# Expert rows gathered by buffer alone: four row buffers, VectorE's row steps tied behind the weight splits

## The chip, the cores and the metric

The kernel runs on one core of one Trainium2 chip. The metric is the device time of one execution in microseconds (us). The time before is 3835.49 us, the median of 3 runs (3828.89 to 3838.25). Engines: TensorE (PE), VectorE (DVE), ScalarE (ACT), GpSimd (POOL) and SyncE (SP); SP, ACT and POOL also issue DMAs, each from its own queue.

## The reference

One decoder block on x of 512 tokens by 2048 features, in float32. Two token mixers run in parallel (a gated causal convolution of 31 taps, and a grouped complex state space model), are gated, merged and projected. Then comes the channel mixer, called PEER, and a final RMS norm:

```
q = h @ w_q;  s = q . sub_keys                 # 8 heads, 2 halves of 128 keys
top 16 of each half; the 256 sums; top 16 of those   -> expert ids (of 16384), gates = softmax
act = gelu(h . u_tab[expert])                  # 8 heads x 16 experts a token
out = sum over experts of gates * act * v_tab[expert]
```

Each token so picks 128 of 16384 experts. An expert is one row of 2048 numbers (8 KB) of `u_tab` and one of `v_tab`; each table has 128 MB.

## The kernel before

**Stages.** Up to about 1412 us the mixers and the routing run: weight pieces of 128x1024 (512 KB) are loaded by SP, split by ACT (high part, line 209) and DVE (low part, line 210), and multiplied by PE as three products. Then comes PEER, which treats the tokens in two ways at once.

**Dense way.** The last 352 tokens (`ND`) are multiplied with *all* experts. `dense_u(j)` makes the gelu of 128 experts' scores (`ga`, from 48 matmuls of 352 columns); `weigh(j, ga)` multiplies it on DVE by the gates of those experts, which `load_gates` brings from DRAM for four `j` at a time into one buffer `gq`, and splits the product; `dense_v(g, dc, ws)` multiplies eight such products with a quarter of the V table (96 matmuls) and DVE adds the sum to `acc`. The first 32 columns of `dense_u` (`LEAD`) run ahead and are reloaded later; after them the loop at line 1243 goes over 16 groups `g` and 4 quarters `dc`. From group 3 to 14 one pass through the inner loop, here called a step, holds two `dense_u`, two `weigh` and one `dense_v`: 192 matmuls and eight weight pieces, taken from the stream `tabs`, which loads up to six and splits up to three pieces ahead.

**Row way.** The first 160 tokens are done by rows. For each token's expert number `e`, `gather_row` has POOL issue an indirect DMA that brings 128 rows of 8 KB, one for each partition (1 MB), into a buffer of the ring `row`; DVE then takes one instruction over 128x2048: for U a product with a sum (line 1113), for V a multiply-add into the result `x` (line 1116). 128 tokens take 128 gathers for each table, and 32 tokens, four partitions to a token, 32 for each: 320 gathers in all. `gather()` is a generator, one row to a `yield`; `pump_rows(n)` advances it by n rows at four places of a step, so that the rows are spread over the dense work. In a step some six rows are taken.

**What sets the order.** The queue of each engine is fixed when the program is built. A scheduler takes the operations in the order of the program where their buffers allow, and may take a later one first. `tc.issue_after(ins)` adds an edge: what is written inside comes behind `ins`. Each queue then runs strictly in order. In the kernel before, a gather is held behind `pace[0]`, an instruction of POOL that was written shortly before it: mostly a copy of one column, `mark`, which `paced` makes from `ga` after a `dense_u` or from `acc` after a `dense_v` (line 1142):

```
        with after(pace[0]):
            nc.gpsimd.indirect_dma_start(out=g, ...)
...
            while len(live) < 2:
                ahead()
```

Three row buffers (`NROW`) hold the row in use and two begun ahead. The ring of `ga` has four buffers (`NR`). The row ring also serves the row way's `xt` and `gain`, the residual `res` in group 0 and `sqj` at the end. `dynamic_dma_scratch_size` reserves 8192 bytes of each partition for the descriptors of POOL's DMAs.

Of the kernel before, what the change touches and what calls it, by code (L numbers as in the profile page):

```python
# [38 lines left out]
LAG = 11  # L39
GM = 1  # L40
TAIL = 5
NR = 4
NROW = 3
RLEAD = 0.8
RV = 0.8
REND = 4.5
# [109 lines left out]
def kernel(ctx, tc, xT, vecs, cst, w_in, conv_w_out, w_vg, w_out, w_q, keysT,  # L156
# [47 lines left out]
        return pp.tile([128, T], F32, name="ps", tag="proj", bufs=4)  # L204

    pace = [None]

    def split(hi, lo, src, eng=None):
        ins = nc.scalar.copy(hi, src).ins  # L209
        low = (eng or nc.vector).tensor_tensor(lo, src, hi.bitcast(F32), op=ALU.subtract)  # L210
        if eng is nc.gpsimd:
            pace[0] = low.ins
        return ins

    rings = {"raw": [(wp, 4)], "hi": [(wp, 3)], "lo": [(wp, 3)]}
# [763 lines left out]

    def weigh(j, ga):  # L980

        if j % QG == 0:
            load_gates(j // QG)
        if j < LEAD:
            ga = gars.pop(j) if j in gars else reload(j)
        g3 = ga.rearrange("p (b t) -> p b t", t=32)
        nc.vector.tensor_tensor(g3, gq[0][:, :, j % QG, :], g3, op=ALU.mult)  # L987
        p = wgp[j // GRP % 2]
        wh, wl = (p.tile([128, ND], F32R, name=n, tag="w") for n in ("wh", "wl"))
        split(wh, wl, ga)  # L990
        return wh, wl

    def reload(j):
# [60 lines left out]

    def gather_row(tab, ids, e):
        g = row("grow")
        with after(pace[0]):
            nc.gpsimd.indirect_dma_start(out=g, out_offset=None, in_=tab,
                                         in_offset=bass.IndirectOffsetOnAxis(ap=ids[:, e:e + 1], axis=0))
        return g  # L1060

    def gather():
        blocks = [(0, GA, eidx, gta, HK, rt[:, 0:1]),
                  (GA, GB, eidb, gtb, HK // REP, rtb)]
        passes = [(b, tab) for b in blocks for tab in (peer_u, peer_v)]
        todo = [(tab, b[2], e) for b, tab in passes for e in range(b[4])]
        live, xt, gain = [], [], []

        def ahead():
            if todo:  # L1070
                live.append(gather_row(*todo.pop(0)))

        def load(b):
            t0, n = b[:2]
            x = row("xt")
            for c in range(128 // n):
                nc.sync.dma_start(x[c * n:(c + 1) * n], d_xr[t0:t0 + n])
            xt.append(x)

        def load_gain():  # L1080
            gain.append(row("gain"))
            nc.gpsimd.dma_start(gain[0], gffn[None, :].to_broadcast([128, D]))

        def turn(scale):
            x2 = rowp.tile([128, D], F32, name="rows0", tag="rows", bufs=1)
            nc.scalar.activation(x2, xt.pop(), AF.Copy, scale=scale)
            return x2

        load(blocks[0])
        load_gain()  # L1090
        for _ in range(3):
            yield
        for p, (b, tab) in enumerate(passes):
            t0, n, ids, gates, steps, r = b
            nxt = passes[p + 1] if p + 1 < len(passes) else (None, None)
            if tab is peer_u:
                x = turn(r)
                ahead()
                _mul(nc, x, x, gain.pop())
            else:  # L1100
                x = turn(float(n) / 128)
            while len(live) < 2:
                ahead()
            for i in range(steps):
                if i == steps - 2 and nxt[0]:
                    load(nxt[0])
                elif i == steps - 1 and nxt[1] is peer_u:
                    load_gain()
                else:
                    ahead()  # L1110
                g = live.pop(0)
                if tab is peer_u:
                    nc.vector.scalar_tensor_tensor(g, g, 1.0, x, op0=ALU.mult, op1=ALU.mult,  # L1113
                                                   accum_out=act[:, i:i + 1])
                else:
                    nc.vector.scalar_tensor_tensor(x, g, act[:, i:i + 1], x, op0=ALU.mult, op1=ALU.add)  # L1116
                yield
            if tab is peer_u:
                with after(last_ga[0]):
                    nc.scalar.activation(act[:, :steps], act[:, :steps], AF.Gelu_apprx_tanh)  # L1120
                _mul(nc, act[:, :steps], act[:, :steps], gates)
                continue
            if n < 128:
                for _ in range(3):
                    yield
                y = row("ysum")
                for q in range(4):
                    pt = ps_v()
                    nc.tensor.matmul(pt[:n], sel, x[:, q * 512:(q + 1) * 512], start=True, stop=True)  # L1129
                    nc.scalar.copy(y[:n, q * 512:(q + 1) * 512], pt[:n])  # L1130
                x = y
            nc.sync.dma_start(out[t0:t0 + n, :], row_norm(x[:n], gfin))
        yield
# [2 lines left out]
    gth = gather()  # L1136
    gi = [0, 0.0]

    def paced(ap):

        mark = con2.tile([128, 1], F32, name="mark", tag="mark", bufs=2)
        pace[0] = nc.gpsimd.tensor_copy(mark, ap[:, 0:1]).ins  # L1142

    def pump_rows(n):
        gi[1] += n
        while gi[0] < gi[1]:
# [4 lines left out]
    for j in range(LEAD):  # L1151
        if j >= LEAD - 4:
            jn = 2 * (j - LEAD + 4)
            gars.update((i, reload(i)) for i in (jn, jn + 1))
        if j == 0:
            rows_load()
        if j in (4, 6):
            rows_turn()
        ga = dense_u(j, gate_steps if j >= LAG else None)
        if j == LAG - 1:  # L1160
            transp_routes()
        if j >= LEAD - 5:
            paced(ga)
            pump_rows(RLEAD)
        if j >= LEAD - 4:
            ws_next += [weigh(jn, None), weigh(jn + 1, None)]
# [50 lines left out]
    def dense_v(g, dc, ws):  # L1217
        pcs = []
        pairs = [ps_v((2, 512)) for _ in range(2)]
        pvs = [pairs[i // 2][:, i % 2, :ND] for i in range(4)]  # L1220
        last = range(GRP - 2, GRP)
        order = [(e, i) for e in range(GRP - 2) for i in range(4)] + [(e, i) for i in range(4) for e in last]
        for at, (e, i) in enumerate(order):
            if at == 16 and g == NE // GRP - 1 and dc:
                turn_out(dc - 1)
            if e // 2 == len(pcs):
                pcs.append(tabs.take())
            hi, lo = pcs[e // 2]
            wh, wl = ws[e]
            s = slice(e % 2 * 512 + i * 128, e % 2 * 512 + (i + 1) * 128)  # L1230
            nc.tensor.matmul(pvs[i], hi[:, s], wh, start=e == 0, stop=False)  # L1231
            nc.tensor.matmul(pvs[i], hi[:, s], wl, start=False, stop=False)  # L1232
            nc.tensor.matmul(pvs[i], lo[:, s], wh, start=False, stop=e == GRP - 1)  # L1233
        for h in range(2):
            a, pv = acc[:, 4 * dc + 2 * h:4 * dc + 2 * h + 2], pairs[h][:, :, :ND]
            _add(nc, a, pv, a if g else res[dc][:, 2 * h:2 * h + 2])
        paced(acc[:, 4 * dc + 3])
        if g == NE // GRP - 1 and dc == 3:
            turn_out(dc)

# [2 lines left out]
    for g in range(ngrp):  # L1243
        ws = ws_next
        ws_next = []
        for dc in range(4):
            if g == ngrp - 1 and dc == 3:
                for _ in gth:
                    pass
            if g == ngrp - 1 and dc == 0:  # L1250
                hst.close()
                op = ctx.enter_context(tc.tile_pool(name="op", bufs=1, reuse_waits="tile"))
                tail["ost"] = op.tile([128, len(BLKS), D], F32, name="ost")
                tail["sqs"] = op.tile([128, len(BLKS), 4], F32, name="sqs")
                tail["gfb"] = op.tile([128, D], F32, name="gfb")
                nc.gpsimd.dma_start(tail["gfb"], gfin[None, :].to_broadcast([128, D]))
            for jn in range((g + 1) * GRP + 2 * dc, (g + 1) * GRP + 2 * dc + 2):
                if jn < NE:
                    ga = None
                    if jn >= LEAD:  # L1260
                        ga = dense_u(jn)
                        paced(ga)
                    ws_next.append(weigh(jn, ga))
                    if jn >= LEAD:
                        pump_rows(rate / 2)
            n = RV / 4 * (3 + (g > 0)) if (g + 1) * GRP < LEAD else rate / 2 if g < ngrp - 1 else REND / 2 if dc < 3 else 0
            if g == 0 and dc < 3:
                load_res()
            pump_rows(n)
            dense_v(g, dc, ws)  # L1270
            pump_rows(n)
# [83 lines left out]
```

## Time and profile before

| | |
|---|---|
| median of 3 runs | 3835.49 us |
| the profiled execution: its own time | 3822.91 us |
| its span, first to last instruction | 3821.1 us |
| busy: PE, DVE, ACT, POOL | 3514.3, 2712.8, 1256.4, 1004.8 us |
| PE, DVE share of the span | 92%, 71% |
| DMA queue of SP: share of 16 engines' span, MB | 35.8%, 437.58 |
| DMA queue of POOL | 27.3%, 396.12 |

The profile is of one execution. A row with a wait names the engine, what it writes and the line, then after an arrow what ended the wait, and the sum, count and longest wait. In a row for a stretch, PEclk is the granted TensorE clock as a share of full speed, and the DMA share is the mean busy share of the 16 DMA engines. Busy shares over the whole span hide that the stages have different limits.

### The profile page before, as it was taken

The page shows a single profiled execution, that of the slowest core. Times are in us where ns is not written, and L with a number is a line of the kernel's source. Part 1 is how long each engine was busy: PE and PEld are TensorE (multiplying, and loading weights), DVE is VectorE, ACT ScalarE, POOL GpSimd, SP SyncE. Part 2 cuts the span into 40 slices and gives each one's busy share as a digit, 9 for nine tenths or more (in the row PEclk, how much of TensorE's full clock was granted, in tenths as well). Part 3 has the DMA queues.
Part 4 walks back from the last instruction along what each step waited for, and adds up shares of the span by engine and source line. Part 5 has one row for each costly group of instructions (what it writes and reads, how often), then busy time and mean ns, then how long its engine had stood idle before and what let it go on. Part 6 is the DMA issues. An engine that isn't in the chain of part 4 may idle for free. (4 is left out here: it accounts for less than half of the span.)

```text
span 3821.1 us, 49889 instructions
## 1 busy us (share of the span) xinstructions
PE 3514.3 (92%) x19059; PEld 3257.5 (85%) x19059; DVE 2712.8 (71%) x4006; ACT 1256.4 (33%) x2009; POOL 1004.8 (26%) x832
## 2 busy tenths in 40 slices
PE   8999999999999999989998998988788888889877
PEld 6888888888888899988998998888788887889877
DVE  8686678985349998756667677676576666767666
ACT  4334434242323348732222222232222222232223
POOL 1100001000025452121233233333343333332331
PEclk9999999999999999999999999999899999999988
DMA  5533444344444356687678888886788767888874
GB/s 184 140 109 115 127 126 143 114 133 140 141 136 121 116 165 208 224 304 254 236 289 301 302 304 306 302 305 245 262 299 292 283 248 267 300 303 308 313 274 182
DMA packets 218863, 852.35 MB, mean 223 GB/s; under 512 B 41168, under 2 KB 58656, under 8 KB 173376
## 3 DMA queue, kind: packets, MB, share of 16 engines
q1 hardware_dynamic: 144704, 437.58, 35.8%
q0 software_dynamic: 64512, 396.12, 27.3%
q10 hardware_dynamic: 9408, 15.47, 1.1%
q8 instruction: 149, 2.44, 0.3%
q14 instruction: 90, 0.74, 0.1%
HBM read 795.23 MB, written 53.84 MB: 222 GB/s over the span
## 5 line engine op out<-in xcount | busy, mean ns | idle before, releaser
L209 ACT CAST whi<-wraw 128x1024 fp32r<-128x1024 f32 x736 | 761.6, 1049 | 1462.4 <-PE ps L269 575.0
L210 DVE TENSOR_TENSOR wlo<-wraw,whi 128x1024 fp32r<-128x1024 f32 x682 | 830.6, 1225 | 227.1 <-ACT whi L209 226.7
L1233 PE MATMUL pv<-wh,wlo 128*128 128x352 f32 x2048 | 707.2, 345 | 178.3 <-DVE wlo L210 178.2
L1231 PE MATMUL pv<-wh,whi 128*128 128x352 f32 x2048 | 704.4, 344 | 34.8 <-DVE acc L61 32.8
L270 PE MATMUL pu<-h2h,wlo 128*128 128x352 f32 x2048 | 676.0, 330 | 50.8 <-DVE wlo L210 50.8
L1232 PE MATMUL pv<-wl,whi 128*128 128x352 f32 x2048 | 696.5, 340 | 0.0
L268 PE MATMUL pu<-h2l,whi 128*128 128x352 f32 x2048 | 681.1, 333 | 1.1 <-ACT whi L209 1.1
L269 PE MATMUL pu<-h2h,whi 128*128 128x352 f32 x2048 | 668.2, 326 | 0.0
L1116 DVE SCALAR_TENSOR_TENSOR rows<-grow,act,rows 128x2048 f32<-128x2048 f32 x160 | 375.7, 2348 | 332.2 <-DMA grow<-in_peer_v_dram,eidx 282.1
L1233 PEld LDWEIGHTS pv<-wh,wlo 128*128 128x128 f32 x2048 | 417.8, 204 | 194.3 <-DVE wlo L210 194.3
L1113 DVE SCALAR_TENSOR_TENSOR grow<-grow,rows 128x2048 f32<-128x2048 f32 x160 | 366.2, 2289 | 277.3 <-DMA grow<-in_peer_u_dram,eidx 227.4
L1231 PEld LDWEIGHTS pv<-wh,whi 128*128 128x128 f32 x2048 | 418.3, 204 | 39.2 <-DVE acc L61 36.0
L270 PEld LDWEIGHTS pu<-h2h,wlo 128*128 128x128 f32 x2048 | 390.7, 191 | 58.1 <-DVE wlo L210 58.0
L1232 PEld LDWEIGHTS pv<-wl,whi 128*128 128x128 f32 x2048 | 419.0, 205 | 0.0
L268 PEld LDWEIGHTS pu<-h2l,whi 128*128 128x128 f32 x2048 | 393.3, 192 | 1.4 <-ACT whi L209 1.4
L269 PEld LDWEIGHTS pu<-h2h,whi 128*128 128x128 f32 x2048 | 391.8, 191 | 0.0
L268 PE MATMUL ps<-hl,whi 128*128 128x512 f32 x896 | 353.2, 394 | 8.7 <-ACT whi L209 8.7
L270 PE MATMUL ps<-hh,wlo 128*128 128x512 f32 x896 | 350.7, 392 | 0.5 <-DVE wlo L210 0.4
L269 PE MATMUL ps<-hh,whi 128*128 128x512 f32 x896 | 350.2, 391 | 0.0
L209 ACT CAST wh<-ga 128x352 fp32r<-128x352 f32 x96 | 46.7, 486 | 834.7 <-DVE ga L987 834.7
L1142 POOL COPY mark<-acc 128x1 f32<-128x1 f32 x64 | 84.5, 1320 | 757.2 <-DVE acc L61 757.2
L1142 POOL COPY mark<-ga 128x1 f32<-128x1 f32 x101 | 97.5, 966 | 506.5 <-ACT ga L916 492.4
(347 smaller groups left out, 5134.0 us busy)
## 6 DMA issues: line engine op xcount, KB each, us to landing
wraw<-in_peer_ut_dram SPq DMA_DIRECT2D x256, 512.0 KB
wraw<-in_peer_vt_dram SPq DMA_DIRECT2D x256, 512.0 KB
wraw<-in_w_in_dram SPq DMA_DIRECT2D x112, 512.0 KB
d_g<-stg SPq DMA_DIRECT2D x22, 1024.0 KB
gq<-d_g POOLq DMA_DIRECT2D x32, 704.0 KB, 11.1
wraw<-in_w_vg_dram SPq DMA_DIRECT2D x32, 512.0 KB
wraw<-in_w_out_dram SPq DMA_DIRECT2D x32, 512.0 KB
wraw<-in_w_q_dram SPq DMA_DIRECT2D x32, 512.0 KB
```

The lines of the kernel that those rows point to most:

```text
L209: ins = nc.scalar.copy(hi, src).ins
L210: low = (eng or nc.vector).tensor_tensor(lo, src, hi.bitcast(F32), op=ALU.subtract)
L268: nc.tensor.matmul(ps, hi[:, sl], al[k], start=k == 0, stop=False)
L269: nc.tensor.matmul(ps, hi[:, sl], ah[k], start=False, stop=False)
L270: nc.tensor.matmul(ps, lo[:, sl], ah[k], start=False, stop=k == nk - 1)
L1113: nc.vector.scalar_tensor_tensor(g, g, 1.0, x, op0=ALU.mult, op1=ALU.mult, accum_out=act[:, i:i + 1])
L1116: nc.vector.scalar_tensor_tensor(x, g, act[:, i:i + 1], x, op0=ALU.mult, op1=ALU.add)
L1142: pace[0] = nc.gpsimd.tensor_copy(mark, ap[:, 0:1]).ins
L1231: nc.tensor.matmul(pvs[i], hi[:, s], wh, start=e == 0, stop=False)
L1232: nc.tensor.matmul(pvs[i], hi[:, s], wl, start=False, stop=False)
L1233: nc.tensor.matmul(pvs[i], lo[:, s], wh, start=False, stop=e == GRP - 1)
```

## The change

The tie `after(pace[0])` is taken off the gathers; their place in POOL's queue follows from their buffer alone. The copies `mark` and `paced` go. `NROW` becomes 4 and three rows are begun ahead. The DVE step of a row is tied behind the last low split that was written before it for DVE (`last_low`). The gates of four columns are loaded right behind the last `weigh` that uses the ones before, no longer at the first that needs them. `NR` becomes 3, and the descriptor scratch 4096 bytes.

```diff
-NR = 4
-NROW = 3
+NR = 3
+NROW = 4
...
         if eng is nc.gpsimd:
             pace[0] = low.ins
+        else:
+            last_low[0] = low.ins
...
     def weigh(j, ga):
-        if j % QG == 0:
-            load_gates(j // QG)
+        if j == 0:
+            load_gates(0)
...
         split(wh, wl, ga)
+        if j % QG == QG - 1 and j + 1 < NE:
+            load_gates(j // QG + 1)
         return wh, wl
...
         g = row("grow")
-        with after(pace[0]):
-            nc.gpsimd.indirect_dma_start(out=g, ...)
+        nc.gpsimd.indirect_dma_start(out=g, ...)
         return g
...
-            while len(live) < 2:
+            while len(live) < NROW - 1:
                 ahead()
...
-                if tab is peer_u:
-                    nc.vector.scalar_tensor_tensor(g, g, 1.0, x, ..., accum_out=act[:, i:i + 1])
-                else:
-                    nc.vector.scalar_tensor_tensor(x, g, act[:, i:i + 1], x, ...)
+                with after(last_low[0]):
+                    if tab is peer_u:
+                        nc.vector.scalar_tensor_tensor(g, g, 1.0, x, ..., accum_out=act[:, i:i + 1])
+                    else:
+                        nc.vector.scalar_tensor_tensor(x, g, act[:, i:i + 1], x, ...)
...
-    def paced(ap):
-        mark = con2.tile([128, 1], F32, name="mark", tag="mark", bufs=2)
-        pace[0] = nc.gpsimd.tensor_copy(mark, ap[:, 0:1]).ins
...
-            paced(ga)
...
-        paced(acc[:, 4 * dc + 3])
...
-                        paced(ga)
...
-    nc = _bacc.Bacc("TRN2", ..., dynamic_dma_scratch_size=8192)
+    nc = _bacc.Bacc("TRN2", ..., dynamic_dma_scratch_size=4096)
```

## Rows read from the trace of the kernel before

**Rows 1.** Stretches: us, busy us (instructions) of PE PEld DVE ACT POOL, PEclk, DMA share, GB/s.
```profile
0.00:1412.00 1412.00, 1390.62 (x6535) 1165.96 (x6536) 1063.81 (x2418) 512.92 (x810) 260.42 (x270) 1.00 0.44 134
1412.00:1691.00 279.00, 267.73 (x1830) 264.72 (x1831) 200.85 (x259) 183.19 (x496) 63.36 (x55) 0.98 0.67 229
1691.00:1887.00 196.00, 178.24 (x1043) 175.91 (x1043) 123.75 (x142) 54.10 (x64) 33.15 (x32) 0.95 0.73 249
1887.00:3722.00 1835.00, 1602.35 (x9222) 1580.33 (x9220) 1263.24 (x1112) 475.52 (x587) 628.63 (x461) 0.93 0.80 290
3722.00:3821.10 99.10, 75.37 (x434) 70.55 (x434) 61.10 (x79) 30.67 (x53) 19.26 (x15) 0.88 0.48 180
```

**Rows 2.** Waits from 1887 to 3722 us: total us, times, longest us.
```profile
POOL mark L1142 <- DVE acc L61: 581.3, 48, 18.6
POOL mark L1142 <- ACT ga L916: 464.9, 49, 13.1
...
DVE rows L1116 <- DMA grow<-in_peer_v_dram,eidx: 282.1, 47, 9.9
...
DVE grow L1113 <- DMA grow<-in_peer_u_dram,eidx: 187.7, 46, 9.6
...
PE pv L1233 <- DVE wlo L210: 177.1, 51, 6.2
...
DVE grow L1113 <- DMA grow<-in_peer_u_dram,eidb: 49.7, 12, 10.5
PE pu L270 <- DVE wlo L210: 46.5, 22, 5.4
...
DVE rows L1116 <- DMA grow<-in_peer_v_dram,eidb: 41.5, 8, 8.3
```

**Rows 3.** POOL in order of time: start us, us, engine, line, operation [wait before].
```profile
2685.45 2.11 POOL L1142 COPY mark<-ga 128x1 f32<-128x1 f32 x1 [10.21 <-ACT ga L916]
2687.71 4.91 POOL L1058 DMA_INDIRECT grow<-in_peer_v_dram,eidx  x1 [0.16 <-DVE wlo L210]
2692.93 0.94 POOL L1058 DMA_INDIRECT grow<-in_peer_v_dram,eidx  x1 [0.30 <-issue]
2694.17 0.94 POOL L1058 DMA_INDIRECT grow<-in_peer_v_dram,eidx  x1 [0.30 <-issue]
2695.11 1.14 POOL L978 DMA_DIRECT2D gq<-d_g  x1
```

**Rows 4.** DVE in the same stretch: the row step that waits.
```profile
2701.41 2.35 DVE L1116 SCALAR_TENSOR_TENSOR rows<-grow,act,rows 128x2048 f32<-128x2048 f32 x1 [8.47 <-DMA grow<-in_peer_v_dram,eidx]
```

**Rows 5.** Groups by line, 1887 to 3722 us: count | busy us, mean ns | wait before.
```profile
L1116 DVE SCALAR_TENSOR_TENSOR rows<-grow,act,rows 128x2048 f32<-128x2048 f32 x150 | 352.2, 2348 | 324.3 <-DMA grow<-in_peer_v_dram,eidx 282.1 <-DMA grow<-in_peer_v_dram,eidb 41.5 <-ACT rows L1086 0.2
L1113 DVE SCALAR_TENSOR_TENSOR grow<-grow,rows 128x2048 f32<-128x2048 f32 x140 | 320.4, 2288 | 237.3 <-DMA grow<-in_peer_u_dram,eidx 187.7 <-DMA grow<-in_peer_u_dram,eidb 49.7
```

**Rows 6.** Two single steps, columns as in the first group.
```profile
3426.00:3460.00 34.00, 29.17 (x164) 28.59 (x163) 29.57 (x29) 7.50 (x10) 11.19 (x9) 0.90 0.95 354
3460.00:3497.00 37.00, 36.78 (x227) 36.49 (x226) 25.76 (x27) 11.90 (x15) 13.47 (x10) 1.00 0.82 298
```

**Rows 7.** Line 1058, 1887 to 3722 us: durations in ns (min/median/max); issue to landing.
```profile
L1058 POOL DMA_INDIRECT grow<-in_peer_v_dram,eidb x23: 945/973/6062, 3571.6 to 3709.7; - x23
...
DMA to landing us min/median/max: 5.7/9.4/15.1
```

**Rows 8.** Waits of SP's queue, whole span.
```profile
SPq L245 <- DVE wlo L210: 2038.4, 474, 14.0
...
SPq L995 <- DVE wl L210: 19.4, 10, 6.5
```

**Rows 9.** Groups by line, 1691 to 1887 us.
```profile
L1231 PE MATMUL pv<-wh,whi 128*128 128x352 f32 x347 | 117.4, 338 | 17.8 <-DVE acc L61 17.8
...
L987 DVE TENSOR_TENSOR gar<-gq,gar 128x352 f32<-128x352 f32 x20 | 9.8, 522 | 8.3 <-DMA gq<-d_g 8.3
```

More of the change, by code (lines that the diff above doesn't have):

```diff
@@ L206 @@
     pace = [None]
+    last_low = [None]
     def split(hi, lo, src, eng=None):
@@ L1056, in gather_row @@
         g = row("grow")
-        with after(pace[0]):
-            nc.gpsimd.indirect_dma_start(out=g, out_offset=None, in_=tab,
-                                         in_offset=bass.IndirectOffsetOnAxis(ap=ids[:, e:e + 1], axis=0))
+        nc.gpsimd.indirect_dma_start(out=g, out_offset=None, in_=tab,
+                                     in_offset=bass.IndirectOffsetOnAxis(ap=ids[:, e:e + 1], axis=0))
         return g
@@ L1111, in gather @@
                 g = live.pop(0)
-                if tab is peer_u:
-                    nc.vector.scalar_tensor_tensor(g, g, 1.0, x, op0=ALU.mult, op1=ALU.mult,
-                                                   accum_out=act[:, i:i + 1])
-                else:
-                    nc.vector.scalar_tensor_tensor(x, g, act[:, i:i + 1], x, op0=ALU.mult, op1=ALU.add)
+                with after(last_low[0]):
+                    if tab is peer_u:
+                        nc.vector.scalar_tensor_tensor(g, g, 1.0, x, op0=ALU.mult, op1=ALU.mult,
+                                                       accum_out=act[:, i:i + 1])
+                    else:
+                        nc.vector.scalar_tensor_tensor(x, g, act[:, i:i + 1], x, op0=ALU.mult, op1=ALU.add)
                 yield
@@ L1341 @@
     laid = _layout(inputs)
-    nc = _bacc.Bacc("TRN2", target_bir_lowering=False, num_devices=1, dynamic_dma_scratch_size=8192)
+    nc = _bacc.Bacc("TRN2", target_bir_lowering=False, num_devices=1, dynamic_dma_scratch_size=4096)
     arrays, args = {}, []
```

## The prediction

> **What bounds the kernel now.** I read the page's shares first: PE 92%, DVE 71%. That looks like a kernel bound by PE, but it is an average. So the second view is busy time by stretch [rows 1]. Up to 1412 us PE is busy 1390.6 of 1412.0 us at a granted clock of 1.00: nothing on the row way can help there. From 1887 to 3722 us, nearly half the span, PE is busy 1602 of 1835 us and its clock is 0.93. This is where the reader should look. The stretch holds 9222 matmuls, and a step has 192, so it holds 48 steps of 38.2 us.
>
> What would a step take if PE never waited? In one step PE was busy 36.78 of 37.00 us at full clock with 227 matmuls [rows 6]: 0.162 us each, so 192 take 31.1 us. A step therefore loses 7.1 us. The third view, who waited for whom in that stretch, says to what [rows 2]. PE waits 177.1 + 46.5 = 223.6 us for `wlo`, a low split by DVE: 4.7 us a step. The remaining 2.4 us are the clock's: it is granted at two levels, 1.2 and 2.4 GHz, the mean is 0.93 in this stretch where PE pauses often, and it was 1.00 in the step without pauses [rows 1, 6].
>
> Why is a DVE that is busy 26.3 us a step (1263.2 / 48) late? Because it also waits 282.1 + 187.7 + 49.7 + 41.5 = 561.0 us for rows to land, 11.7 us a step [rows 2]. 26.3 + 11.7 = 38.0 of 38.2 us: **DVE either works or waits for a row**, and the splits that PE needs stand behind the waiting row in its queue. It is DVE's queue that sets the step, not its work.
>
> The fourth view, POOL and DVE in order of time, shows why rows come late [rows 3, 4]. POOL waits 10.2 us for the `ga` that its mark copies, and then three gathers go out at once, at 2687.7, 2692.9 and 2694.2. DVE needs the first of them at once and stands 8.5 us until it lands, starting at 2701.4. In the 1835 us marks waited 581.3 us for `acc` and 464.9 us for `ga` [rows 2]: the gathers follow DVE's and PE's progress, DVE follows the gathers, and PE follows DVE. It is a loop with the landing time in it (median 9.4 us, longest 15.1) [rows 7].
>
> **The change, part by part.**
>
> *Gathers untied, fourth buffer.* A gather now needs only the end of the row step four before it. A step takes 290 / 48 = 6.04 rows [rows 5]. At a step of 33.4 us (below) rows come every 5.5 us, so a gather has 4 x 5.5 - 2.35 = 19.8 us before its row is wanted, and the median landing takes 9.4 us and the longest 15.1 [rows 7]. On the mean this covers the landing; two rows in a bunch eat some of the 10 us of slack. I take the 11.7 us of waiting as gone, except for what POOL itself costs.
>
> *What is late next.* Without that wait DVE needs 26.3 us and PE 31.1. But POOL's issue gets dearer as DVE pauses less. A gather takes 0.94 us when DVE stands still, and one that was issued into a run of DVE work took 4.91 [rows 3]; the longest took 6.06 [rows 7]. Suppose that POOL only gets on while DVE pauses: per step 6.04 gathers x 0.95 plus half a gates' load of 1.14 [rows 3] are 6.3 us, and 26.3 + 6.3 = 32.6 us. If issues overlapped freely the bound would be PE's 31.1; if every one took 6.06, with 0.30 between them, 6.04 x 6.36 + 0.57 = 39.0. I take 32.6: most gathers now last between the two, and a row that comes late for this reason itself makes the pause in which POOL catches up. PE then idles 1.5 us a step and not 4.7, a third, so I leave a third of the clock's loss, 0.8 us. **A step of 33.4 us**, and 48 x (38.2 - 33.4) = 230 us saved.
>
> The Trainium skill, "SBUF — State Buffer", section "SBUF: two separate sides", has a rule here that speaks against the change: a DMA from GpSimd's queue stalls, because its descriptors cannot be written, for as long as DVE runs an operation that takes both of its ports. The 4.91 us against 0.94 [rows 3] agree in direction; whether the stall is complete they do not show. By the rule no step below 32.6 us is possible, since every gather would have to be written in DVE's pauses; without it PE's 31.1 would stand and the saving would be some 330 us.
>
> *VectorE's steps behind the last split.* It costs no instruction. It puts the splits that were written before a row ahead of it, so a late row no longer holds these; up to three split pieces of 24 matmuls, 3 x 3.9 = 11.7 us, then stand ready for PE. The other side: a row that has landed waits where the split in front of it waits for `ga` or for a piece that PE still holds. Four places a step would have to cost 2.9 us each to eat the present 11.7. I take 0, as DVE has 31.1 - 26.3 = 4.8 us of slack a step, and such a wait means that DVE is ahead of PE.
>
> *Marks removed, gates' load moved.* The marks are POOL work beside everything; their cost was their wait. The gates' load (1.14 us on POOL, every second step) now stands right behind the last use of the old gates, and gathers behind it wait for a multiply of DVE. That costs at most a wait like the mark's, 10.2 us [rows 3], once in two steps, under a lead of 19.8; I take 0. In exchange the 8.3 us go that DVE waits for gates [rows 9].
>
> *Groups 0 to 2* (1691 to 1887 us). 1043 matmuls x 0.162 = 169 of 196 us, and PE waits 17.8 us for `acc` behind DVE's late rows [rows 1, 9]. Fewer rows fall here, so I take half of the 27 us lost: 13. Three `ga` buffers for four make SP wait one reload sooner; SP waited 19.4 us for these in all, off PE's path, as the weight stream waits much longer for DVE (2038 us) anyway [rows 8]. I take 0; +19 if it came on the path, or nothing.
>
> *Scratch of 4 KB.* The trace does not show how full it is. Before 1412 us PE's idle time is 21 us in all, so POOL's DMAs are hidden there; I take 0, with 20 us either way. From 1412 to 1691 and behind 3722 us (few rows left, PE busy 75 of 99) I take 0, with 20 us to be gained at most [rows 1].
>
> **Sum.** 230 + 13 = 243 us. The profiled execution took 3822.9 (span 3821.1), and becomes 3580. The median of the runs shown lies 12.6 above it, so I predict **3592 us**.
>
> **Rivals.**
>
> *PE's floor is reached.* Issues overlap well and rows are always there: a step of 31.3, 48 x 6.9 = 331, with 20 more in the groups before: 3485 us. For it: four buffers give twice the median landing time. Against it: the long issues.
>
> *The DMA engines become the bound.* A step moves 290 GB/s x 38.2 us = 11.1 MB [rows 1]; in 33.4 us that is 332 GB/s, at a share of 0.92 instead of 0.80. One step ran at 354 and 0.95, with eight rows, in 34.0 us [rows 6], but one step is no stretch, and gathers with more in flight slow the weights. If the share stops at 0.87, a step takes 38.2 x 0.80 / 0.87 = 35.1 us; 48 x 3.1 = 149, and 8 before: 3678 us.
>
> By the Trainium skill, "DMA: Bandwidth & Descriptors", section "Specifications", the HBM gives one core some 358 GB/s; an estimate by it is 11.1 / 0.358 = 31 us a step, so it would not bind above PE's floor. The 354 GB/s of that one step agree.
>
> *It doesn't do what it says.* Buffers come free in bunches, because row steps come in bunches and the gates' load holds POOL for DVE; the gathers still go out three at a time, DVE still stands for the first, and the loop closes over the buffers in place of the marks. Against it: in the waits of today [rows 2, 3] the gathers go at once when the mark is there, so their buffers were free before. Price 0: 3835.
>
> *Slower: POOL's issue becomes the bound.* With DVE nearly always at work each gather takes as long as the longest now. 39.0 us a step (above) is 0.8 over today's, so 3835 + 37 = 3872 us. It decides from a mean issue of (38.2 - 0.57) / 6.04 - 0.30 = 5.9 us. For it: 4.91 and 6.06 are there already. Against it: POOL is busy only 628.6 / 48 = 13.1 us a step, marks included [rows 1], and with every late row DVE pauses.
>
> **Chances.** Forecast (steps of 32 to 34.5 us) 0.52, PE's floor 0.13, DMA 0.19, nothing 0.07, slower 0.09. About 0.3%, some 12 us, is what a measurement of this kernel can tell from no change. Faster by more: 0.52 + 0.13 + 0.19 = 0.84; within: 0.07; slower: 0.09. The range goes from PE's floor, 3480, past the DMA case to 3730, where the bounds of 20 us each lie inside; what it leaves out is nothing, slower and a little of each end.
>
> **What would show it.** Right: between the same groups a step of 33 to 34 us; DVE's wait for rows under 3 us a step; PE's wait for `wlo` a third of 224 us, clock above 0.96; gathers spread over the step and not in threes; their median issue above 1.5 us. DMA case: a share of 0.87 to 0.9, PE and ACT waiting for `wraw`. Slower case: POOL busy over 30 us a step. I am wrong if DVE still waits 8 us for rows at one place of each step, or if it waits for the splits in front of them instead.

## The result: 3470 us, and the profile after

The changed kernel takes 3470.27 us, the median of 4 runs (3465.20 to 3472.65), beside 3832.19 us for the kernel before (4 runs). The ratio is 0.9059 (0.9030 to 0.9088): 362 us less, where I forecast 243 less and put the low end of the range at 3480. The direction was right, the size was not. The profiled execution took 3465.2 us.

The page of the kernel after, span and busy times with their shares:

```profile
span 3463.4 us, 49577 instructions
...
PE 3384.4 (98%) x19059; PEld 3151.0 (91%) x19059; DVE 2709.3 (78%) x4006; ACT 1276.2 (37%) x2009; POOL 905.3 (26%) x667
```

DVE has the same work as before (2712.8 us), in a shorter span. Busy time by stretch, columns as in [rows 1]; group 3 begins at 1886 us (before: 1887) and group 15 at 3377 (before: 3722):

```profile
1886.00:3377.00 1491.00, 1486.55 (x9219) 1486.25 (x9218) 1269.60 (x1115) 495.51 (x586) 546.26 (x318) 1.00 0.93 356
...
3377.00:3463.40 86.40, 70.65 (x430) 65.87 (x428) 59.87 (x78) 30.59 (x53) 10.82 (x8) 0.95 0.50 193
```

| | before | after | difference |
|---|---|---|---|
| up to group 3 | 1887 | 1886 | -1 |
| groups 3 to 14, 48 steps | 1835 | 1491 | -344 |
| from group 15 on | 99.1 | 86.4 | -13 |

All but 14 us of the gain lies in the 48 steps. One takes 1491 / 48 = 31.06 us, and PE is busy 30.97 of them at a clock of 1.00: it is PE's floor. The waits of that stretch, columns as in [rows 2]:

```profile
POOL grow L1062 <- DVE rows L1121: 453.4, 144, 11.8
ACT whi L210 <- PE pv L1231: 448.2, 188, 9.1
POOL grow L1062 <- DVE grow L1118: 420.2, 83, 14.4
...
DVE wlo L211 <- ACT whi L210: 169.0, 100, 2.6
...
DVE grow L1118 <- DMA grow<-in_peer_u_dram,eidb: 5.7, 3, 4.8
...
PE pv L1232 <- DVE wlo L211: 4.5, 1, 4.5
...
DVE rows L1121 <- DMA grow<-in_peer_v_dram,eidx: 2.3, 2, 1.6
```

DVE's waits for rows fell from 561.0 us to 5.7 + 2.3 = 8.0, PE's waits for `wlo` from 223.6 to 4.5 (I had left it a third). The arrows have turned: POOL waits for DVE to free a row buffer, DVE for ACT's high part, and ACT for PE to free a piece. Everybody waits for PE. POOL and then DVE in order of time, columns as in [rows 3]:

```profile
2225.98 0.94 POOL L1062 DMA_INDIRECT grow<-in_peer_u_dram,eidx  x1 [3.60 <-DVE grow L1118]
2228.99 1.68 POOL L1062 DMA_INDIRECT grow<-in_peer_u_dram,eidx  x1 [2.07 <-DVE grow L1118]
2238.23 2.75 POOL L1062 DMA_INDIRECT grow<-in_peer_u_dram,eidx  x1 [7.56 <-DVE grow L1118]
```

```profile
2226.43 2.28 DVE L1118 SCALAR_TENSOR_TENSOR grow<-grow,rows 128x2048 f32<-128x2048 f32 x1
...
2228.64 2.35 DVE L211 TENSOR_TENSOR wlo<-wraw,whi 128x1024 fp32r<-128x1024 f32 x2
2233.01 1.23 DVE L211 TENSOR_TENSOR wlo<-wraw,whi 128x1024 fp32r<-128x1024 f32 x1 [2.01 <-ACT whi L210]
2234.15 0.52 DVE L990 TENSOR_TENSOR ga<-gq,ga 128x352 f32<-128x352 f32 x1
2235.22 0.53 DVE L211 TENSOR_TENSOR wl<-ga,wh 128x352 fp32r<-128x352 f32 x1 [0.55 <-ACT wh L210]
2235.66 2.29 DVE L1118 SCALAR_TENSOR_TENSOR grow<-grow,rows 128x2048 f32<-128x2048 f32 x1
```

Each gather goes as soon as a row step has freed its buffer. On DVE the splits and the multiply of `ga` now stand in front of the next row step, and no row step waits: answer to [rows 4].

### The profile page after: what moved, and what is told of

It is laid out like the page before. It is cut to its first block, busy times and chain, and to the rows that moved or that the text cites. A ratio compares the mean times of both kernels' runs of the same rounds, so it can differ in the third digit from the quotient of the medians.

```text
span 3463.4 us, 49577 instructions
## 1 busy us (share of the span) xinstructions
PE 3384.4 (98%) x19059; PEld 3151.0 (91%) x19059; DVE 2709.3 (78%) x4006; ACT 1276.2 (37%) x2009; POOL 905.3 (26%) x667
## 4 chain that ended last, share of the span: by engine, by line
PE 80%; DVE 12%; DMA 3%; issue 3%; POOL 1%; ACT 1%; SPq 0%; DVEq 0%; ACTq 0%; POOLq 0%
PE ps L271 9%; PE pu L272 9%; PE ps L273 9%; PE ps L272 9%; PE pu L273 8%; PE pu L271 8%; PE pv L1230 8%; PE pv L1232 8%; PE pv L1231 8%; PE pv L967 2%; DVE acc L476 2%; DMA gar<-d_ga 1%; DVE wlo L211 1%; DMA gq<-d_g 1%; DVE oh L834 1%
## 5 line engine op out<-in xcount | busy, mean ns | idle before, releaser
L273 PE MATMUL pu<-h2h,wlo 128*128 128x352 f32 x2048 | 663.5, 324 | 25.0 <-POOL wlo L211 24.3
L1230 PE MATMUL pv<-wh,whi 128*128 128x352 f32 x2048 | 669.5, 327 | 13.7 <-DVE acc L61 12.3
L1232 PE MATMUL pv<-wh,wlo 128*128 128x352 f32 x2048 | 663.0, 324 | 6.5 <-DVE wlo L211 6.5
L271 PE MATMUL pu<-h2l,whi 128*128 128x352 f32 x2048 | 667.7, 326 | 0.6 <-ACT whi L210 0.6
L1231 PE MATMUL pv<-wl,whi 128*128 128x352 f32 x2048 | 661.1, 323 | 0.0
L1230 PEld LDWEIGHTS pv<-wh,whi 128*128 128x128 f32 x2048 | 386.8, 189 | 16.5 <-DVE acc L61 13.8
L1232 PEld LDWEIGHTS pv<-wh,wlo 128*128 128x128 f32 x2048 | 386.9, 189 | 7.4 <-DVE wlo L211 7.4
L1231 PEld LDWEIGHTS pv<-wl,whi 128*128 128x128 f32 x2048 | 389.2, 190 | 0.0
L1062 POOL DMA_INDIRECT grow<-in_peer_u_dram,eidx x128 | 227.3, 1776 | 491.3 <-DVE grow L1118 441.2
L1062 POOL DMA_INDIRECT grow<-in_peer_v_dram,eidx x128 | 218.3, 1705 | 404.1 <-DVE rows L1121 386.4
L271 PEld LDWEIGHTS ps<-hl,whi 128*128 128x128 f32 x896 | 169.0, 189 | 45.5 <-ACT whi L210 9.2
```

Of the source, the lines that this page charges most:

```text
L271: nc.tensor.matmul(ps, hi[:, sl], al[k], start=k == 0, stop=False)
L273: nc.tensor.matmul(ps, lo[:, sl], ah[k], start=False, stop=k == nk - 1)
```

## The experiments

Theory A, as the expectations call it, is the prediction's: the marks make the rows late, and untying the gathers is what brings the gain. Theories B and C, in the first expectations, give the gain to the fourth buffer and to the tie on DVE. Theory D was formed when A fell: two locks hold the same step. One is the mark on the gather; the other is the place of the row step in DVE's queue, ahead of splits and multiplies that PE and the next mark need. Each kernel is told as an edit of the kernel after or before; differences are against the kernel before on the same chip.

**Marks back, all else as after.**

```diff
-        nc.gpsimd.indirect_dma_start(out=g, ...)
+        with after(pace[0]):
+            nc.gpsimd.indirect_dma_start(out=g, ...)
...
+            paced(ga)
...
+        paced(acc[:, 4 * dc + 3])
```

> The changed kernel with one part undone: the gathers are tied to POOL's marks again, the copies of one column of ga and acc are back; four buffers, three rows ahead, the tie on DVE and the early gates stay. Theory A (the loop through the marks made the rows late; untying is the gain): most of the gain goes, 3720 to 3835 us, POOL waits for ga and acc at its marks, DVE again waits 6 us or more a step for rows. Theory B (the fourth buffer is the gain): under 3560 us, DVE's wait for rows under 3 us a step. Theory C (the tie that puts splits ahead of rows is the gain): under 3600 us, DVE may wait for rows but PE's wait for low splits stays small.

Measured: 3480.23 us, ratio 0.9060 (0.9036 to 0.9084), 356 us less. Theory A falls: the marks can stay. B and C both fit this time. From 1850 to 3300 us PE is busy 1445.7 of 1450 us, though marks still wait (waits of that stretch):

```profile
POOL mark L1148 <- DVE acc L61: 318.3, 48, 13.6
POOL mark L1148 <- ACT ga L919: 250.1, 75, 6.1
...
DVE rows L1122 <- DMA grow<-in_peer_v_dram,eidx: 11.7, 7, 2.6
```

Marks wait 568 us, and DVE next to nothing for rows.

**Three row buffers, all else as after.**

```diff
-NROW = 4
+NROW = 3
```

> The changed kernel with three row buffers and two rows begun ahead; all else as changed. Theory A: a gather now has three row intervals of 5.1 us less one row step of 2.35, 13 us, against a median landing of 9.4 us: near the floor, 3480 to 3560 us, DVE waits 0.5 to 3 us a step for rows, more where two rows come in a bunch. Theory B: the gain goes, above 3650 us, DVE waits 6 us or more a step. Theory C: as A.

Measured: 3481.00 us, 0.9067 (0.9043 to 0.9090). Theory B falls. DVE does wait for rows again, and it costs PE hardly anything (1850 to 3300 us, waits; PE is busy 1439.7 of the 1450 us):

```profile
DVE rows L1121 <- DMA grow<-in_peer_v_dram,eidx: 44.7, 37, 3.1
DVE grow L1118 <- DMA grow<-in_peer_u_dram,eidx: 39.8, 26, 2.7
...
DVE grow L1118 <- DMA grow<-in_peer_u_dram,eidb: 14.8, 10, 4.0
```

The waits are short (4.0 us at most, 10.5 before), some 2.2 us a step in all, and lie in DVE's own slack of 31.0 - 26.4 = 4.6 us a step.

**No tie on VectorE, all else as after.**

```diff
-                with after(last_low[0]):
-                    if tab is peer_u:
...
+                if tab is peer_u:
...
```

> The changed kernel without the tie of DVE's row step behind the last low split; all else as changed. Theory A: rows are there when they are wanted, so it matters little which stands first: 3465 to 3510 us. Theory C: row steps stand ahead of splits again, and a late row holds PE: above 3560 us, with PE waiting over 60 us for low splits between 1850 us and the end.

Measured: 3543.08 us, 0.9230 (0.9205 to 0.9254): 70 us of the gain are gone though the gathers are free. That lies between the ranges of A and C. The row steps run ahead of their places until the gates' load holds POOL; then the gathers behind it stand. The stretches, and the waits from 2250 us on:

```profile
1850.00:2250.00 400.00, 388.38 (x2381) 386.19 (x2381) 379.83 (x377) 120.56 (x146) 165.18 (x106) 0.99 1.00 396
2250.00:3300.00 1050.00, 1025.57 (x6320) 1021.67 (x6319) 797.86 (x672) 334.71 (x405) 287.40 (x181) 0.99 0.84 316
```

```profile
POOL gq L981 <- DVE ga L990: 240.5, 6, 61.2
```

Up to 2250 us 99 gathers go out in 12.4 steps, 8 a step for 6, DVE works 380 of 400 us and the DMA share is 1.00. Later POOL stands before a gates' load for up to 61 us at a time, no gather passes, and DVE works 798 of 1050 us. These rows explain only a part: the profiled execution is 78 us longer than that of the kernel after, and by the count of matmuls some 41 of these lie before group 3 (where PE waits 29.5 us for `acc`, in the kernel after 12.3), 33 in the 48 steps and 4 behind them. That the bunches of rows are what PE loses this time by was not tested by itself.

**Gates loaded late, all else as after.**

```diff
-        if j == 0:
-            load_gates(0)
+        if j % QG == 0:
+            load_gates(j // QG)
...
-        if j % QG == QG - 1 and j + 1 < NE:
-            load_gates(j // QG + 1)
```

> The changed kernel with the gates' load back at the first column that needs them; all else as changed. If the early load does nothing: 3460 to 3480 us. If the load now stands in POOL's queue behind gathers that wait for their buffers (they wait some 1000 us in all in the changed kernel), gates land up to 10 us late every second step, DVE's multiply waits for them, and the splits behind it: 24 x 5 to 10 us of DVE waiting, of which the 4.8 us of slack a step hide most: 3480 to 3580 us, and DVE shows a wait for gq.

Measured: 3475.74 us, 0.9056 (0.9033 to 0.9079). The early load is worth nothing that these runs can tell.

**The tie alone, on the kernel before.**

```diff
-                if tab is peer_u:
...
+                with after(last_low[0]):
+                    if tab is peer_u:
...
```

> The kernel before plus the tie of DVE's row step behind the last low split, nothing else (marks, three buffers, late gates stay). New theory D: in the kernel before a row step stood in DVE's queue ahead of the multiply and the splits that were written before it, while its gather waited for a mark made from the acc or ga of the same place; breaking either end of this loop is enough. D: 3475 to 3560 us, DVE waits under 4 us a step for rows, although the gathers still follow the marks. Theory A (untying the gathers from the marks is the gain): 3750 to 3840 us. Theory B' (with marks, it takes the fourth buffer too): 3600 to 3750 us.

Measured: 3576.71 us, 0.9336 (0.9289 to 0.9382), 258 us less with marks, three buffers and all else as before: 17 us above D's range and below those of B' and A. A row step in DVE's order of time, before (first) and with the tie (second):

```profile
2217.07 2.35 DVE L210 TENSOR_TENSOR wlo<-wraw,whi 128x1024 fp32r<-128x1024 f32 x2
2227.26 2.29 DVE L1113 SCALAR_TENSOR_TENSOR grow<-grow,rows 128x2048 f32<-128x2048 f32 x1 [7.83 <-DMA grow<-in_peer_u_dram,eidx]
...
2229.48 0.52 DVE L987 TENSOR_TENSOR ga<-gq,ga 128x352 f32<-128x352 f32 x1
```

```profile
2216.27 0.53 DVE L990 TENSOR_TENSOR ga<-gq,ga 128x352 f32<-128x352 f32 x1 [1.05 <-POOL mark L1146]
2217.35 0.53 DVE L211 TENSOR_TENSOR wl<-ga,wh 128x352 fp32r<-128x352 f32 x1 [0.55 <-ACT wh L210]
2219.75 2.29 DVE L1117 SCALAR_TENSOR_TENSOR grow<-grow,rows 128x2048 f32<-128x2048 f32 x1 [1.88 <-DMA grow<-in_peer_u_dram,eidx]
```

Before, the multiply of `ga` stands behind the row that waits 7.83 us. With the tie it has gone ahead, and the row has had that much longer to land. This is the second lock, and I had priced it at 0. It isn't the whole: the waits from 1850 to 3300 us are

```profile
DVE rows L1120 <- DMA grow<-in_peer_v_dram,eidx: 106.0, 70, 6.6
...
DVE grow L1117 <- DMA grow<-in_peer_u_dram,eidx: 83.2, 42, 4.9
```

With 11.1 us for the rows of `eidb` that is 200.3 us, 4.6 us a step for 11.7 before; D had asked for under 4.

**The gathers untied alone, on the kernel before.**

```diff
-        with after(pace[0]):
-            nc.gpsimd.indirect_dma_start(out=g, ...)
+        nc.gpsimd.indirect_dma_start(out=g, ...)
...
-            paced(ga)
...
-        paced(acc[:, 4 * dc + 3])
```

> The kernel before with the gathers untied and the marks gone, nothing else (three buffers, no tie on DVE, late gates). D and A: the loop is open, 3500 to 3620 us; without the tie on DVE rows run ahead of their places, as they did in the changed kernel without the tie, so some 70 us worse than with it. Theory B (lead from the fourth buffer is needed when the row steps are not tied): above 3650 us, DVE waits over 5 us a step.

Measured: 3630.19 us, 0.9473 (0.9434 to 0.9513), 204 us less. Untying is worth much alone, but not all, and less than the tie. The time is 10 us above the range of A and D and below that of B; DVE still waits 3.1 us a step for rows, and POOL up to 61.1 us before a gates' load, as in the variant without the tie.

**Four buffers with the marks, on the kernel before** (`NR` 3 and 4 KB of scratch to pay for the buffer).

```diff
-            while len(live) < 2:
+            while len(live) < NROW - 1:
```

> The kernel before with four row buffers and three rows begun ahead, paid with three ga buffers and 4 KB of scratch; marks stay, no tie on DVE, late gates. D: one more row begun ahead of its use means that the row DVE wants was issued at a mark before, about half a step earlier, so the wait goes as well: 3500 to 3640 us. Theory A: the gathers still follow the marks, 3750 to 3840 us.

Measured: 3822.77 us (10 runs), 0.9978 (0.9959 to 0.9997): 12 us. Here D, as I had put it, was wrong, and A's number was met. DVE still stands as long (DVE, then POOL, in order of time):

```profile
2183.82 2.35 DVE L210 TENSOR_TENSOR wlo<-wraw,whi 128x1024 fp32r<-128x1024 f32 x2
2196.03 2.29 DVE L1113 SCALAR_TENSOR_TENSOR grow<-grow,rows 128x2048 f32<-128x2048 f32 x1 [9.87 <-DMA grow<-in_peer_u_dram,eidx]
```

```profile
2184.03 1.04 POOL L1142 COPY mark<-acc 128x1 f32<-128x1 f32 x1 [11.11 <-DVE acc L61]
2185.23 1.78 POOL L1058 DMA_INDIRECT grow<-in_peer_u_dram,eidx  x1 [0.16 <-issue]
```

A buffer more doesn't open the loop by itself: the gathers still go after the mark, and DVE has 2.35 us of work between the `acc` that frees the mark and the next row step. It gives a lead once one of the two locks is off (the table below).

**`NR` 3 and the small scratch alone, on the kernel before.**

```diff
-NR = 4
+NR = 3
...
-dynamic_dma_scratch_size=8192
+dynamic_dma_scratch_size=4096
```

> The kernel before with only what paid for the fourth buffer: three ga buffers in place of four and 4 KB of descriptor scratch in place of 8. All theories: within 0.5% of the kernel before, 3820 to 3850 us. If the scratch limits POOL's transfers: the gathers' issues get longer than the 1.27 and 0.97 us median of before and the time rises by 10 us or more.

Measured: 3836.61 us (10 runs), 1.0015 (0.9996 to 1.0035): nothing, as priced.

**The first four gathers tied, all else as after.** In the kernel after, PE loses 24.3 us at once before group 0. POOL in order of time:

```profile
1398.35 1.05 POOL L1062 DMA_INDIRECT grow<-in_peer_u_dram,eidx  x1 [29.25 <-DVE ef L858]
1399.43 3.50 POOL L211 TENSOR_TENSOR wlo<-wraw,whi 128x1024 fp32r<-128x1024 f32 x1
```

and PE's waits from 1380 to 1887 us:

```profile
PE pu L273 <- POOL wlo L211: 24.3, 1, 24.3
PE pv L1230 <- DVE acc L61: 12.3, 5, 6.5
```

The first gather, freed of its mark, was put ahead of low splits that POOL makes in this stage; it waits 29.25 us for the expert numbers, and the splits behind it wait too. So:

```diff
+        with after(pace[0] if first_rows else None):
+            if first_rows:
+                first_rows.pop()
             nc.gpsimd.indirect_dma_start(out=g, ...)
```

> The changed kernel, but its first four gathers are again tied behind POOL's last instruction before them. In the changed kernel the scheduler put them at 1398 us into POOL's queue, where the first waits 29 us for the experts' numbers and holds POOL's low splits, and PE waits 24.3 us for one of these. If that wait is time lost on the path: 3440 to 3455 us. If the stretch up to the first row steps has slack that takes it up again: 3465 to 3475 us.

Measured: 3454.15 us (5 runs), 0.9018 (0.8997 to 0.9039), the lowest of the kernels that do all the work; the interval overlaps that of the kernel after by a little, and the traces show the 15 us: group 3 begins at 1871 us for 1886, and the wait is gone. PE's waits in the same stretch:

```profile
PE pu L273 <- DVE wlo L211: 8.9, 3, 4.1
```

**VectorE made fuller, all else as after.** This one is for my sum: a multiply over 128x512 more for each row fills DVE's pauses.

```diff
+                _mul(nc, g[:, :512], g[:, :512], g[:, :512])
```

> The changed kernel with one more DVE instruction behind each row step, a multiply over 128x512 of the row that is done with (about 0.68 us by such instructions in the trace, 4.1 us a step, so DVE is at work 30.4 of 31.0 us). It measures whether POOL's issues need DVE's pauses, the price that the prediction put into its step. If they do (26.3 + 4.1 + 6.3 = 36.7 us a step): about 3745 us, DVE waits for rows. If POOL gets on beside DVE: 3465 to 3500 us, issues longer than 1.74 us on the mean, but no wait for rows.

Measured: 3481.68 us, 0.9093 (0.9066 to 0.9119). By my sum a step would be 26.3 + 4.1 + 6.3 = 36.7 us, some 3745 in all; it stays at PE's floor with DVE at work 1374.9 of 1450 us (1850 to 3300 us: the stretch, then the costliest of POOL's groups by line, columns as in [rows 5]):

```profile
1850.00:3300.00 1450.00, 1443.22 (x8937) 1442.35 (x8936) 1374.89 (x1354) 478.50 (x564) 633.56 (x300) 1.00 0.92 350
```

```profile
L1062 POOL DMA_INDIRECT grow<-in_peer_v_dram,eidx x128 | 371.9, 2906 | 265.0 <-DVE grow L53 241.3 <-issue 12.8 <-DVE act L53 6.1
```

DVE pauses 75 us in 1450, and POOL spends 371.9 + 169.9 + 51.3 + 20.3 = 613 us on 276 issues (the four groups of line 1062), 2.22 us each. Even at 0.94 us each, 259 us, they would not fit into the pauses. The issues lie beside DVE's work, only longer.

**Two dense products for three, all else as after.** To see what stands below PE's floor, the first of the three products of `dense_u` and the second of `dense_v` are left out, a third of the step's matmuls.

```diff
-            nc.tensor.matmul(ps, hi[:, sl], al[k], ...)
...
-            nc.tensor.matmul(pvs[i], hi[:, s], wl, ...)
```

> The changed kernel with one of the three products left out in the dense way (the one with the low part of the activations; so the output is less exact there). PE then needs some 20.6 us a step, and the step shows what lies next below PE's floor. If it is DVE (26.3 us of work): steps of 26.5 to 28 us, DMA at 395 to 415 GB/s, 3180 to 3320 us. If it is the DMA engines at the 355 GB/s of the changed kernel: steps stay at 30 to 31 us, 3400 to 3470 us. If rows again come late: DVE waits over 3 us a step for them.

Measured: 3210.43 us, 0.8374 (0.8349 to 0.8398). The stretch 2000 to 2600 us:

```profile
2000.00:2600.00 600.00, 504.39 (x2820) 493.13 (x2819) 574.90 (x509) 221.17 (x266) 294.67 (x145) 0.90 1.01 404
```

2820 matmuls of 128 a step are 22.0 steps of 27.2 us. So neither DVE with its rows, nor POOL, nor the DMA engines hold the kernel after at 31 us. At 27.2 us DVE works 96% of the time and the DMA share is 1.01; which of these two ends it there was not separated.

**The parts together.** Medians, with the difference from the kernel before:

| tie on DVE | gathers untied | four buffers | us | difference |
|---|---|---|---|---|
| | | x | 3822.77 | -12 |
| | x | | 3630.19 | -204 |
| | x | x (early gates) | 3543.08 | -294 |
| x | | | 3576.71 | -258 |
| x | | x (early gates) | 3480.23 | -356 |
| x | x | (early gates) | 3481.00 | -356 |
| x | x | x (all) | 3470.27 | -362 |

Alone the three sum to -474, together they give -362: PE's floor cuts the rest. The fourth buffer is worth 12 us alone, but 90 where the gathers are untied (204 to 294) and 98 with the tie (258 to 356), the early gates counted in; with both it is worth 6. With the tie either of the other two suffices to come within 11 us of the whole; without it neither, nor both.

## Why the prediction was wrong

**What held.** The step of 192 matmuls at 0.162 us, 31.1 us, was right within 0.04. DVE's queue set the step, and 26.4 us of DVE work a step came out for 26.3. Of what I said would show it, this came: DVE's waits for rows 8.0 / 48 = 0.2 us a step (I asked for under 3), the clock 1.00 (over 0.96), the gathers spread, their median issue 1.68 to 1.79 us (over 1.5). The step of 33 to 34 us didn't, nor a third of PE's wait for `wlo`: 4.5 us of 224 are left. The scratch, `NR` and the gates' load cost nothing, as priced (3836.61 and 3475.74 us).

**The step that failed: "what is late next".** I let POOL get on only while DVE pauses and made 26.3 + 6.3 = 32.6 us of it. The two don't add: from 1886 to 3377 us the four groups of gathers hold 218.3 + 198.8 + 59.5 + 42.9 = 519.5 us in 292 issues, 1.78 us each and 10.8 us a step; with 26.4 us of DVE they lie in 31.06 us. Even at 0.94 us each, 274 us, the issues would not fit into DVE's pauses, 1491 - 1269.6 = 221 us. In the fuller variant 29.5 us of DVE and 13.2 of issues a step lie in 31.15 us. The issue lengthens beside DVE's work (0.94 us alone, up to 2.91 in the kernel after and 6.55 in the fuller variant), but goes on. With it fell the 0.8 us of low clock, which hung on PE's idling by 1.5 us. Together that is 33.4 - 31.06 = 2.34 us a step, 48 x 2.34 = 112 us: the miss between the profiled executions is 115 (358 for 243). The medians miss by 122, as I put the median 12.6 us above the profiled execution and it lies 5.1 above.

The rule that I set beside it I had also taken too widely. The Trainium skill, "SBUF — State Buffer", section "Who interferes with whom", gives the complete stall for copies, casts and `tensor_scalar`; a `tensor_tensor` with both inputs in SBUF, it says, contends with GpSimd's reads only. DVE's work here is mostly `tensor_tensor` and `scalar_tensor_tensor`, which the section does not name, and the runs agree that it doesn't shut POOL out: 276 issues in the fuller variant's 1450 us, with 75 us of pauses. The price of 1.78 us is the runs' alone.

The trace of before had shown it, and I read only the two long issues, of 4.91 and 6.06 us. POOL and DVE of the kernel before, 2234 to 2240 us:

```profile
2233.97 1.78 POOL L1058 DMA_INDIRECT grow<-in_peer_u_dram,eidx  x1 [0.16 <-DVE grow L1113]
2236.05 1.88 POOL L1058 DMA_INDIRECT grow<-in_peer_u_dram,eidx  x1 [0.30 <-issue]
2238.24 1.27 POOL L1058 DMA_INDIRECT grow<-in_peer_u_dram,eidx  x1 [0.30 <-issue]
```

```profile
2233.70 1.22 DVE L210 TENSOR_TENSOR wlo<-wraw,whi 128x1024 fp32r<-128x1024 f32 x1
2234.83 2.28 DVE L1113 SCALAR_TENSOR_TENSOR grow<-grow,rows 128x2048 f32<-128x2048 f32 x1
2237.04 0.08 DVE L1113 DVE_READ_ACCUMULATOR grow<-grow,rows 128x1 f32 x1
2237.04 0.52 DVE L987 TENSOR_TENSOR ga<-gq,ga 128x352 f32<-128x352 f32 x1
2237.48 1.22 DVE L210 TENSOR_TENSOR wlo<-wraw,whi 128x1024 fp32r<-128x1024 f32 x1
2238.62 0.52 DVE L210 TENSOR_TENSOR wl<-ga,wh 128x352 fp32r<-128x352 f32 x1
2239.07 1.23 DVE L210 TENSOR_TENSOR wlo<-wraw,whi 128x1024 fp32r<-128x1024 f32 x1
```

No row of DVE has a wait in brackets, and three issues of 1.78, 1.88 and 1.27 us begin and end in that time. These rows forbid "only while DVE pauses" and give the price as 1.3 to 1.9 us beside DVE's work. They show how it comes about, too: each issue ends 0.9 us behind the start of DVE's next instruction (2234.83, 2237.04 and 2238.62 us), as if it were held for the instruction that runs when it begins and no longer. In the kernel after, this holds for 215 of the 291 issues from 1890 to 3377 us; 45 began beside DVE's add of `acc`, which has one input in PSUM, and took 0.93 to 0.95 us; most of the rest were held for a second or third instruction. So an issue needs the end of a DVE instruction, not a pause.

**The tie, "I take 0".** I gave all 11.7 us to the untying and the buffer. These do take the waits away (without the tie 43 us are left from 1850 us to the end), but only 294 us of the time. The tie alone is worth 258 us and the untying alone 204. It did no harm to the sum, since the waits went and the floor was reached, but a reader who kept the untying and dropped the tie would have lost 70 us. I had read that the splits stand behind the waiting row [rows 4] and did not ask what moving them alone would do.

**Groups 0 to 2, -13.** Up to group 3 the kernel gained 1 us; with the first four gathers tied, 1871 for 1887, -16. The term was right (by the count of matmuls the groups take 184 us for 196, -12) and hidden by the 24.3 us in which PE waited for a split that stood behind the first gather on POOL, which made the stretch before group 0 some 10 us longer. I had counted the untied gathers in the steady stretch and not asked what the first of them would be put in front of in POOL's queue.

**The rest.** The tail gave 13 us where I took 0: PE idled 15.8 us there for 23.7, at a clock of 0.95 for 0.88. The rival "PE's floor" (3485) had 31.3 us a step for 31.06, which is 11.5 us, and no tail; so 3480 as the low end was the floor with nothing below it, and the time fell 10 us under. Its chance of 0.13 was low because of two long issues. The DMA rival is refuted: a share of 0.93 at 356 GB/s in the kernel after, and 1.01 at 404 with two products. The slower rival asked for a mean issue of 5.9 us; it is 1.78.

## What to carry to other kernels

Where one engine waits for a transfer and another for what stands behind it, look at what is queued behind the wait as well as at what starts the transfer: reordering the queue and starting the transfer earlier are two cures for one loop. Try each alone before one is credited: once the next bound is reached, the other has little left to give. Before two engines' times are added because they disturb each other, look for a stretch in which one of them never pauses and see what the other did there, and at which of its instructions the other got on. An operation freed of its tie may be put in front of work that it used to stand behind: look at its first instance too.

## What the runs showed of the hardware

A gather's issue on POOL took 0.94 us with DVE still, 1.78 us on the mean with DVE at work 85% of the time (1269.6 of 1491 us), and 2.22 us at 95%. Beside DVE's work on inputs in SBUF most issues ended 0.9 us behind the end of the DVE instruction that they began beside; beside the add of `acc` from PSUM they took 0.93 to 0.95 us (45 issues). The 16 DMA engines moved 396 GB/s for 400 us (the variant without the tie) and 404 GB/s for 600 us (two products), both at a share of 1.00 to 1.01; the step of [rows 6] had shown 354, and the some 358 GB/s that the prediction quotes are exceeded. The Trainium skill, "DMA: Bandwidth & Descriptors", section "Bandwidth", calls that the share of a core while both cores of a memory domain stream, and gives 425 GB/s for one alone; these runs on one core, at 404, lie above the first and 5% below the second.
